# Layer 1 MLP of a diffusion backbone: the seven products of a pair in another order, and the low parts of the second weights made by an accumulating DMA

## The chip, the cores and the metric

The kernel runs on one core of one Trainium2 chip. The metric is the device time of one execution in microseconds (us), from the first to the last instruction of the core plus what the launch adds. The core has five engines that each run their own list of instructions strictly in order: PE (TensorE, matrix products), DVE (VectorE), ACT (ScalarE), POOL (GpSimd) and SP (SyncE, which here only issues DMAs). They wait for one another through semaphores. Sixteen DMA engines move data; SP and POOL issue into queues of their own.

## The reference, cut to what matters

Two groups of tokens (512 latent, 128 context, here joined to T = 640 columns) run through two layers. Each layer is a mixer and then an MLP; the change touches only the MLP of layer 1:

```python
def squared_relu_mlp(h, w1, w2):          # h (640, 1024), w1 (1024, 4096), w2 (4096, 1024)
    a = jax.nn.relu(h @ w1)
    return (a * a) @ w2
...
        x = x + g2 * squared_relu_mlp(h, w_ff1[l], w_ff2[l])
```

All data are float32. The kernel gets the precision by splitting each operand in two: a high part, which is the value rounded to the engine's float32r format, and a low part, which is the value less its high part.

## The kernel before

**Three matmuls for one.** `mm3` (lines 798 to 803) multiplies two split operands: high weights by high data (L801), high weights by low data (L802), low weights by high data (L803). So each weight tile is an SBUF tile `w` of 128 partitions by 2 by 1024: `w[:, 0]` high, `w[:, 1]` low. L803 is the only one of the three that reads the low part of the weights.

**Weights.** A `Weights` object `st` holds one list of weight tiles in the order of use. `loads` issues SP DMAs from DRAM into five buffers `raw` of 512 KB. `pump` takes the next item of the list: ACT rounds `raw` into the high part (L214) and DVE subtracts it from `raw` into the low part (L216). `need` returns a tile and pumps until it is there. `free` gives its place back. In this stage there are six places for converted tiles (eight, less two that hold sums of inputs): an item that finds no free place is not pumped, however often `pump` is called.

**The MLP of layer 1.** The 4096 hidden columns are worked in 8 blocks of 512 (`b` = 0 to 7). Blocks 0 and 1 make their hidden activations in the ordinary way before the stage that changes. For blocks 2 to 7, `up7` makes a pair of 128-column tiles, f and g, with two pairs to a block. It is a seven-product scheme in the manner of Strassen: the 2 by 2 products over the two halves of the 1024 inputs and the two halves of the tokens (`C1`, 320 columns each) are formed by 7 products in place of 8. Each product is 4 `mm3`, so 12 matmuls of 320 columns. Its weights ("w1s", items 0 to 6 of a pair) are f and g pieces or their sums, made by `w1s_use`: ACT rounds (L558), DVE makes the low part (L559), and for some items DVE then works the next combination into `raw` (L563). Two items share one place. `p1`, `u2`, `u3` are partial sums that ACT (L1598) and DVE (L1581) take out of the PSUM banks `pa`, `pb`, `pc`, `pd`; four of the products accumulate a second time into a bank that has been read. `finish` squares the rectified result into the split activations `aa`: ACT Relu (L1586), ACT Square (L1587), ACT Copy to the high part (L1588), DVE low part (L1589).

After its two pairs, a block's `down` multiplies its four activation tiles with the second weights and adds the result to `x` (L1407). Its 16 results (8 of rows `d`, 2 of columns) take 192 matmuls. The second weights of a block are four "w2" items, (k, h) with k = 0 or 2 and h the half of the output rows; all four places are taken while the block's `down` runs, and the two left are for w1s items. `blocks7` starts the block's `down` with "early" parts: the first two rows d for both column halves, on the first pair's activations alone (24 matmuls), then the second pair's part of them.

The order on each engine is the order in which this code issues instructions; `pump` calls, written by hand, place the conversions between the others.

Of the kernel before, what the change touches and what calls it, by code (L numbers as in the profile page):

```python
# [136 lines left out]
class Weights:  # L137
# [3 lines left out]
    def __init__(self, nc, raw):  # L141
        self.nc, self.raw = nc, raw
        self.items, self.loaded, self.done = [], 0, 0
        self.raw_live, self.raw_cap, self.tiles, self.of = 0, RAWB, {}, {}
        self.raws = {}
        self.slots = None
        self.caps = {}
        self.lo = nc.vector
        self.own = {}
        self.hold = None  # L150
        self.slow = ()
        self.later, self.skip = [], False
        self.keep, self.second = {}, None

# [39 lines left out]
    def pump(self, n=1):  # L194
# [4 lines left out]
        while n > 0 and self.done < len(self.items):  # L199
# [8 lines left out]
            if use is None:  # L208
                if own is None:
                    self.of[key], w = self.slots.take([128, 2, 1024], F32R)  # L210
                else:
                    w = own()
                r = ts[0][:, 0:size]
                self.nc.scalar.activation(out=w[:, 0, 0:size], in_=r, func=AF.Copy)  # L214
                lo = self.nc.gpsimd if key[0] in self.slow else self.lo
                lo.tensor_tensor(  # L216
                    out=w[:, 1, 0:size], in0=r, in1=w[:, 0, 0:size].bitcast(F32), op=ALU.subtract
                )
# [50 lines left out]
def body(ctx, tc, a):  # L269
# [278 lines left out]
    def w1s_use(l, b, p, i):  # L548


        def use(ts):
            if i == 0:
# [3 lines left out]
            src = (f0, g0, g0, f0, f1, g1, f1)[i]  # L556
# [4 lines left out]
                    4: (f1, f1, g0, ALU.subtract)}.get(i)  # L561
# [15 lines left out]
    def add_w2h(l, b):  # L577
        for h in range(2):
            for k in (0, 2):
                st.add(("w2", l, b, k, h), [(rows(a["w_ff2"][l], b * FB + k, 2, h * 512, 512), (2, 512))], 1024)  # L580
# [866 lines left out]
    def mlp(l, C, H, lead, CL, per_d, per_c, mid, tick=None, turn=None, seven=False):  # L1447
# [107 lines left out]
        def up7(b, p):  # L1555
            n = C[0][1]

            def product(i, op, ps, first):
# [9 lines left out]
                st.free(("w1s", l, b, p, i))  # L1568
# [14 lines left out]
            def finish(j, ci, src=None):  # L1583
                c = slice(*C[ci])
                r, aa = rs[j][:, c], A[b, j]
                act(out=r, in_=r if src is None else src, func=AF.Relu)  # L1586
                act(out=r, in_=r, func=AF.Square)  # L1587
# [11 lines left out]
            st.pump()  # L1599
            pd = product(1, 2, None, True)  # L1600
            st.pump()
# [9 lines left out]
            pa = product(4, (0, 1), pa, False)  # L1611
            lo()
            lo = finish(f, 0, pa)
            if not p:
                st.pump()
            pd = product(5, 3, pd, False)
# [3 lines left out]
            pc = product(6, (1, 1), pc, False)  # L1620
# [3 lines left out]
            lo()  # L1624
            if not p:
                st.pump()

        def blocks7(f0):

            for b in range(NFB):  # L1630
# [9 lines left out]
                if b < NFB - 1:  # L1640
                    early = cut(range(2), C) if b >= f0 else []
                    todo = [(d, c, None) for d in range(2 if early else 0, KD) for c in C]
                    for j, (d, c, ps) in enumerate(early + todo):
# [5 lines left out]
                        if j % 2 or j > 3:  # L1649
# [537 lines left out]
```

## Time and profile before

| | us |
|---|---|
| runs, median (lowest to highest of 3) | 1299.65 (1296.63 to 1301.23) |
| profiled execution, device time | 1302.88 |
| its span | 1301.1 |
| PE busy | 1261.8 (97%) |
| DVE busy | 826.6 (64%) |
| ACT busy | 549.3 (42%) |
| POOL busy | 216.5 (17%) |

The profiled execution is one run of its own, 3.2 us above the median of the others. PE is busy 97% of the span, with the caution that matmuls are pipelined and a record is longer than the distance to the next one. The stage that the change touches runs from about 960 us to the end.

### The profile page before, as it was taken

What the parts mean: (1) busy time and instruction counts of PE and PEld (TensorE: products, weight loads), DVE (VectorE), ACT (ScalarE), POOL (GpSimd) and SP (SyncE); (2) the same over time, 40 slices, a digit from 0 to 9 for tenths busy, and PEclk for the clock granted to TensorE, in tenths of its full rate; (3) what the DMA queues carried; (4) which work ended last, traced back from release to release, by engine and by line L of the source; (5) the groups of instructions that cost most, each with busy time, mean ns of one, the idle gap of its engine ahead of it and who ended that gap; (6) DMA issues with size and microseconds to landing.
All of it is one profiled execution on the core that took longest, in us unless ns stands there. A gap on an engine that the chain in (4) does not pass through costs nothing.

```text
span 1301.1 us, 20746 instructions
## 1 busy us (share of the span) xinstructions
PE 1261.8 (97%) x8308; PEld 1183.4 (91%) x8308; DVE 826.6 (64%) x1553; ACT 549.3 (42%) x993; POOL 216.5 (17%) x182
## 2 busy tenths in 40 slices
PE   7999999999999999999999999799999999999997
PEld 5899975689999999999999998789999999999997
DVE  5753864564766575666666638876887567675664
ACT  4445454453453434333343414534235435354353
POOL 0010312221113221313131315610000000000001
PEclk8999999999999999999999999899999999999999
DMA  7742286340335344444353431202113223132102
GB/s 291 261 164 72 81 227 234 131 170 25 116 117 160 113 145 131 150 126 157 119 161 114 147 130 33 97 1 79 52 35 112 80 67 98 38 111 84 61 33 82
DMA packets 63200, 149.89 MB, mean 115 GB/s; under 512 B 5072, under 2 KB 21968, under 8 KB 62592
## 3 DMA queue, kind: packets, MB, share of 16 engines
q1 hardware_dynamic: 61360, 142.53, 33.3%
q0 software_dynamic: 1456, 5.96, 1.9%
q8 instruction: 65, 1.06, 0.3%
q14 instruction: 31, 0.25, 0.1%
q10 hardware_dynamic: 288, 0.08, 0.0%
HBM read 140.02 MB, written 5.39 MB: 112 GB/s over the span
## 4 chain that ended last, share of the span: by engine, by line
PE 79%; DVE 10%; ACT 7%; issue 2%; DMA 1%; POOL 0%; DVEq 0%; ACTq 0%; POOLq 0%
PE dn_ps L802 11%; PE dn_ps L801 11%; PE dn_ps L803 11%; PE up_ps L801 7%; PE up_ps L803 7%; PE up_ps L802 7%; PE wo_ps L801 1%; PE o_ps L1302 1%; PE wo_ps L803 1%; PE wo_ps L802 1%; ACT r L1587 1%; DVE w L216 1%; ACT w L558 1%; ACT r L1586 1%; PE t_ps L1269 1%
## 5 line engine op out<-in xcount | busy, mean ns | idle before, releaser
L801 PE MATMUL dn_ps<-aa,w 128*128 128x320 f32 (+4 forms) x1024 | 319.1, 312 | 2.1 <-ACT aa L1588 2.1
L802 PE MATMUL dn_ps<-aa,w 128*128 128x320 f32 (+4 forms) x1024 | 318.4, 311 | 0.7
L803 PE MATMUL dn_ps<-aa,w 128*128 128x320 f32 (+4 forms) x1024 | 316.8, 309 | 0.0
L802 PE MATMUL up_ps<-h,w 128*128 128x320 f32 (+2 forms) x800 | 248.6, 311 | 6.0 <-DVE h L752 5.9
L801 PE MATMUL up_ps<-h,w 128*128 128x320 f32 (+2 forms) x800 | 249.6, 312 | 1.3 <-ACT h L748 1.3
L803 PE MATMUL up_ps<-h,w 128*128 128x320 f32 (+2 forms) x800 | 248.6, 311 | 0.0
L1407 DVE SCALAR_TENSOR_TENSOR x<-dn_ps,mod,x 128x320 f32<-128x320 f32 (+4 forms) x360 | 144.7, 434 | 115.0 <-PE dn_ps L803 113.2
L801 PEld LDWEIGHTS dn_ps<-aa,w 128*128 128x128 f32 x1024 | 193.1, 189 | 5.8 <-ACT aa L1588 4.1
L216 DVE TENSOR_TENSOR w<-raw,w 128x1024 fp32r<-128x1024 f32 (+4 forms) x122 | 151.3, 1250 | 70.9 <-ACT w L214 69.8
L802 PEld LDWEIGHTS dn_ps<-aa,w 128*128 128x128 f32 x1024 | 193.0, 188 | 2.5 <-DVE aa L1589 2.4
L803 PEld LDWEIGHTS dn_ps<-aa,w 128*128 128x128 f32 x1024 | 193.0, 189 | 0.0
L214 ACT ACTIVATE w<-raw 128x1024 fp32r<-128x1024 f32 (+4 forms) x131 | 132.0, 1026 | 112.0 <-DMA raw<-w_ff 85.0
L802 PEld LDWEIGHTS up_ps<-h,w 128*128 128x128 f32 x800 | 151.2, 189 | 8.1 <-DVE h L752 8.1
L801 PEld LDWEIGHTS up_ps<-h,w 128*128 128x128 f32 x800 | 151.0, 189 | 4.9 <-issue 3.4
L466 POOL TENSOR_TENSOR acc<-acc,raw 128x1024 f32<-128x1024 f32 x42 | 100.7, 2399 | 303.7 <-ACT raw L464 297.6
L803 PEld LDWEIGHTS up_ps<-h,w 128*128 128x128 f32 x800 | 151.0, 189 | 0.0
L559 DVE TENSOR_TENSOR w<-raw,w 128x512 fp32r<-128x512 f32 x84 | 57.7, 687 | 34.6 <-ACT w L558 33.7
L558 ACT ACTIVATE w<-raw 128x512 fp32r<-128x512 f32 x84 | 51.4, 624 | 61.9 <-DVE raw L563 57.1
L464 ACT ACTIVATE raw<-raw,cs 128x1024 f32<-128x1024 f32 x42 | 48.3, 1149 | 62.6 <-DVE acc L459 54.2
L1925 POOL TENSOR_TENSOR y<-y,fg 128x1024 f32<-128x1024 f32 x1 | 2.4, 2392 | 416.5 <-ACT y L1921 416.5
L1481 DVE TENSOR_TENSOR r<-r,up_ps 128x328 f32<-128x328 f32 (+2 forms) x80 | 37.6, 484 | 42.6 <-ACT r L1480 41.0
L1484 DVE TENSOR_TENSOR aa<-r,aa 128x640 fp32r<-128x640 f32 (+3 forms) x52 | 39.6, 762 | 35.6 <-ACT aa L1483 35.6
(404 smaller groups left out, 2122.1 us busy)
## 6 DMA issues: line engine op xcount, KB each, us to landing
raw<-w_ff SPq DMA_DIRECT2D x126, 512.0 KB, 3.6
raw<-w_mod SPq DMA_DIRECT2D x80, 512.0 KB, 3.9
raw<-w_m SPq DMA_DIRECT2D x16, 512.0 KB, 6.0
raw<-w_out SPq DMA_DIRECT2D x8, 512.0 KB, 4.4
kT<-ckvT POOLq DMA_DIRECT2D x4, 768.0 KB, 10.8
xr<-x SPq DMA_DIRECT2D x5, 512.0 KB, 5.5
xs<-x SPq DMA_DIRECT2D x2, 1280.0 KB, 9.3
x<-xs POOLq DMA_DIRECT2D x2, 1280.0 KB, 9.6
```

The source lines that it names most:

```text
L214: self.nc.scalar.activation(out=w[:, 0, 0:size], in_=r, func=AF.Copy)
L216: lo.tensor_tensor(out=w[:, 1, 0:size], in0=r, in1=w[:, 0, 0:size].bitcast(F32), op=ALU.subtract)
L464: act(out=raw if k else acc[1], in_=raw, func=AF.Copy, scale=w[1])
L466: nc.gpsimd.tensor_tensor(out=acc[1], in0=acc[1], in1=raw, op=ALU.add)
L558: act(out=w[:, 0], in_=src, func=AF.Copy)
L559: vec.tensor_tensor(out=w[:, 1], in0=src, in1=w[:, 0].bitcast(F32), op=ALU.subtract)
L801: mm(ps, lhsT=st_[0], rhs=mv[0], start=first, stop=False, skip_group_check=on)
L802: mm(ps, lhsT=st_[0], rhs=mv[1], start=False, stop=False, skip_group_check=on)
L803: mm(ps, lhsT=st_[1], rhs=mv[0], start=False, stop=last, skip_group_check=on)
L1407: vec.scalar_tensor_tensor(out=xv, in0=ps[:, p0:p0 + c1 - c0], scalar=gate[:, d, m:m + 1], in1=xv, op0=ALU.mult, op1=ALU.add)
L1481: vec.tensor_tensor(out=rv, in0=rv, in1=ps, op=ALU.mult)
L1484: vec.tensor_tensor(out=aa[:, 1, lo:hi], in0=r[:, lo:hi], in1=aa[:, 0, lo:hi].bitcast(F32), op=ALU.subtract)
```

## The change

It does five things, all in layer 1's MLP.

1. **Low parts of w2.** For the 32 w2 items (4 in each of 8 blocks), DVE's subtraction is gone. ACT writes the negated high part into the low part's place, and POOL then issues a DMA that adds the weights from DRAM onto it. The `raw` buffer is still loaded, for the high part.
2. **Order of the products.** The accumulating products come as pd, pc, pa in place of pa, pd, pc; so the items 4, 5 and 6 of a pair have other sources, and the last `finish` of a pair is that of (f, first columns).
3. **Pumps.** Two `pump` calls at a pair's start go, others move. In `down`, the 14 calls of a block are those with j > 1. A w1s item is freed one product later than before.
4. **`finish` from PSUM.** The product that is finished straight from PSUM is squared by DVE (Relu times PSUM) in place of ACT.
5. **Early parts** take the second half of the columns first.

```diff
@@ class Weights, pump
                 self.nc.scalar.activation(out=w[:, 0, 0:size], in_=r, func=AF.Copy)
+                if key in self.add_lo:
+                    self.nc.scalar.activation(
+                        out=w[:, 1, 0:size], in_=w[:, 0, 0:size].bitcast(F32), func=AF.Copy, scale=-1.0
+                    )
+                    src, shape = loads[0]
+                    v = w[:, 1, 0:size].rearrange("p (k n) -> p k n", k=shape[0])
+                    self.nc.gpsimd.dma_start(out=v, in_=src, accum_op=ALU.add)
                 lo = self.nc.gpsimd if key[0] in self.slow else self.lo
-                lo.tensor_tensor(
-                    out=w[:, 1, 0:size], in0=r, in1=w[:, 0, 0:size].bitcast(F32), op=ALU.subtract
-                )
+                if key not in self.add_lo:
+                    lo.tensor_tensor(
+                        out=w[:, 1, 0:size], in0=r, in1=w[:, 0, 0:size].bitcast(F32), op=ALU.subtract
+                    )
@@ w1s_use
-            src = (f0, g0, g0, f0, f1, g1, f1)[i]
+            src = (f0, g0, g0, f0, g1, g0, f1)[i]
...
-                    4: (f1, f1, g0, ALU.subtract)}.get(i)
+                    4: (g0, f1, g0, ALU.subtract)}.get(i)
@@ up7, product
-                st.free(("w1s", l, b, p, i))
+                gone.append(("w1s", l, b, p, i))
+                if i:
+                    st.free(gone.pop(0))
@@ up7, finish
-                act(out=r, in_=r if src is None else src, func=AF.Relu)
-                act(out=r, in_=r, func=AF.Square)
+                if src is not None:
+                    act(out=r, in_=src, func=AF.Relu)
+                    vec.tensor_tensor(out=r, in0=r, in1=src, op=ALU.mult)
+                else:
+                    act(out=r, in_=r, func=AF.Relu)
+                    act(out=r, in_=r, func=AF.Square)
@@ up7
             pa = product(0, (0, 0), None, True)
             p1 = new("p1")
             act(out=p1, in_=pa, func=AF.Copy)
-            st.pump()
             pd = product(1, 2, None, True)
-            st.pump()
             pb = product(2, 1, None, True)
...
-            pa = product(4, (0, 1), pa, False)
-            lo()
-            lo = finish(f, 0, pa)
-            if not p:
-                st.pump()
-            pd = product(5, 3, pd, False)
+            pd = product(4, 3, pd, False)
             add(out(g, 0), u2, pd)
             lo()
             lo = finish(g, 0)
-            pc = product(6, (1, 1), pc, False)
+            if not p:
+                st.pump()
+            pc = product(5, (1, 1), pc, False)
             add(out(f, 1), u2, pc)
             lo()
             lo = finish(f, 1)
-            lo()
             if not p:
                 st.pump()
+            pa = product(6, (0, 1), pa, False)
+            lo()
+            finish(f, 0, pa)()
+            st.free(gone.pop(0))
@@ blocks7
-                    early = cut(range(2), C) if b >= f0 else []
+                    early = cut(range(2), C[::-1]) if b >= f0 else []
...
-                        if j % 2 or j > 3:
+                        if j > 1:
                             st.pump()
```

In the built program the instructions come in another order on ACT and DVE. The rows below are of one block (b = 5) and its second pair; the other blocks from 2 to 7 read alike. Line numbers of the changed program are 10 to 20 higher than before: L215 is the old L214, L567 the old L558, L568 and L572 the old L559 and L563, L1596 the old L1581, L1606 to L1609 the old L1586 to L1589, L1618 the old L1598; L217 is the negated copy, L1603 and L1604 the Relu and the product of the new `finish`.

ACT before, from the second pair's `p1`: `w_11157`, `w_11177`, `w_11197` and `w_11221` are the four w2 tiles of the block, `up_ps` are PSUM banks, `r` and `aa` a tile before and after the split.

```order
L1598 ACTIVATE p1_11155<-up_ps_11142 128x320
L214 ACTIVATE w_11157<-raw_10687 128x1024
L214 ACTIVATE w_11177<-raw_10907 128x1024
L214 ACTIVATE w_11197<-raw_10909 128x1024
L1586 ACTIVATE r_11141<-r_11141 128x320
L1587 ACTIVATE r_11141<-r_11141 128x320
L1588 ACTIVATE aa_11140<-r_11141 128x320
L214 ACTIVATE w_11221<-raw_11136 128x1024
L1586 ACTIVATE r_11139<-up_ps_11142 128x320
```

ACT in the change, at the end of the same pair: `w_11200` holds the last two w1s items, `w_11276` and `w_11311` are the first two w2 tiles, and L1603 is the Relu of the pair's last product.

```order
L567 ACTIVATE w_11200<-raw_10803 128x512
L1606 ACTIVATE r_11154<-r_11154 128x320
L1607 ACTIVATE r_11154<-r_11154 128x320
L1608 ACTIVATE aa_11153<-r_11154 128x320
L1606 ACTIVATE r_11152<-r_11152 128x320
L1607 ACTIVATE r_11152<-r_11152 128x320
L1608 ACTIVATE aa_11151<-r_11152 128x320
L1603 ACTIVATE r_11152<-up_ps_11155 128x320
L1608 ACTIVATE aa_11151<-r_11152 128x320
L215 ACTIVATE w_11276<-raw_10816 128x1024
L217 ACTIVATE w_11276<-w_11276 128x1024
L215 ACTIVATE w_11311<-raw_10941 128x1024
```

Before, three of the four w2 tiles are converted near the start of the pair and the fourth before the last products; in the change the first stands behind the finish of the pair's last product.

DVE before, in the same pair: the low parts of the w2 tiles (L216) stand among the sums of products (L1581).

```order
L216 TENSOR_TENSOR w_11157<-raw_10687,w_11157 128x1024
L216 TENSOR_TENSOR w_11177<-raw_10907,w_11177 128x1024
L1581 TENSOR_TENSOR u2_11193<-p1_11155,up_ps_11180 128x320
L1581 TENSOR_TENSOR u3_11194<-u2_11193,up_ps_11164 128x320
L216 TENSOR_TENSOR w_11197<-raw_10909,w_11197 128x1024
L1581 TENSOR_TENSOR r_11141<-u3_11194,up_ps_11204 128x320
L216 TENSOR_TENSOR w_11221<-raw_11136,w_11221 128x1024
L1589 TENSOR_TENSOR aa_11140<-r_11141,aa_11140 128x320
```

DVE in the change, from the end of the first pair (`w_11111` holds items 3 and 4 of the second pair, `raw_10801` is the buffer in which combinations are made) to the second pair's `u3`:

```order
L568 TENSOR_TENSOR w_11111<-raw_10801,w_11111 128x512
L1596 TENSOR_TENSOR r_11022<-u2_11066,up_ps_11074 128x320
L1609 TENSOR_TENSOR aa_11023<-r_11024,aa_11023 128x320
L568 TENSOR_TENSOR w_11111<-raw_10803,w_11111 128x512
L572 TENSOR_TENSOR raw_10801<-raw_10803,raw_10801 128x4x128
L1609 TENSOR_TENSOR aa_11021<-r_11022,aa_11021 128x320
L1604 TENSOR_TENSOR r_11022<-r_11022,up_ps_11025 128x320
L1609 TENSOR_TENSOR aa_11021<-r_11022,aa_11021 128x320
L1596 TENSOR_TENSOR u2_11196<-p1_11168,up_ps_11183 128x320
L1596 TENSOR_TENSOR u3_11197<-u2_11196,up_ps_11170 128x320
```

The w2 subtractions are gone from DVE, and the first pair's conversions and low parts now stand ahead of the second pair's `u2` and `u3`; `u3` reads the bank `up_ps_11170`, into which the product right behind it accumulates again.

POOL had nothing to do in this stage before. In the change it has 32 rows such as these four of the block:

```order
L222 DMA w_11276<-w_ff2 128x2x512
L222 DMA w_11311<-w_ff2 128x2x512
L222 DMA w_11338<-w_ff2 128x2x512
L222 DMA w_11353<-w_ff2 128x2x512
```

Each waits for ACT's negated copy of its tile.

## Rows read from the trace of the kernel before

**Rows 1.** Head of the page: busy time of each engine (share, instructions).

```profile
PE 1261.8 (97%) x8308; PEld 1183.4 (91%) x8308; DVE 826.6 (64%) x1553; ACT 549.3 (42%) x993; POOL 216.5 (17%) x182
```

**Rows 2.** Timeline of PE in block 4's `down`: start, length, line, tiles.

```profile
1100.31 0.31 PE L803 MATMUL dn_ps<-aa,w 128*128 128x320 f32 x1
...
1121.86 0.31 PE L803 MATMUL dn_ps<-aa,w 128*128 128x320 f32 x1
```

**Rows 3.** Timeline of PE: the same place in blocks 5 and 6 (wait in brackets).

```profile
1153.54 0.41 PE L801 MATMUL dn_ps<-aa,w 128*128 128x320 f32 x1 [0.26 <-ACT aa L1588]
...
1207.58 0.42 PE L801 MATMUL dn_ps<-aa,w 128*128 128x320 f32 x1 [0.27 <-ACT aa L1588]
```

**Rows 4.** Waits of PE from 960 to 1280 us: total, times, longest.

```profile
PE up_ps L801 <- DVE u L1581: 2.4, 2, 1.5
PE dn_ps L801 <- ACT aa L1588: 2.1, 7, 0.6
PE up_ps L801 <- DVE x L1407: 0.5, 1, 0.5
```

**Rows 5.** Timeline of DVE at the end of block 4's second pair.

```profile
1092.97 0.48 DVE L1581 TENSOR_TENSOR r<-u,up_ps 128x320 f32<-128x320 f32 x1
1095.94 1.23 DVE L216 TENSOR_TENSOR w<-raw,w 128x1024 fp32r<-128x1024 f32 x1 [2.49 <-ACT w L214]
```

**Rows 6.** ACT's groups, 1019 to 1235 us: count, busy, mean ns, idle before.

```profile
L558 ACT ACTIVATE w<-raw 128x512 fp32r<-128x512 f32 x57 | 34.9, 625 | 45.2 <-DVE raw L563 41.4 <-PE dn_ps L803 3.8
L214 ACT ACTIVATE w<-raw 128x1024 fp32r<-128x1024 f32 x16 | 16.0, 1048 | 0.0
L1588 ACT ACTIVATE aa<-r 128x320 fp32r<-128x320 f32 x32 | 15.1, 472 | 1.0
...
L1598 ACT ACTIVATE p<-up_ps 128x320 f32<-128x320 f32 x9 | 3.9, 429 | 63.0 <-PE up_ps L803 63.0
L1586 ACT ACTIVATE r<-up_ps 128x320 f32<-128x320 f32 x8 | 3.4, 419 | 0.0
```

**Rows 7.** DVE's groups in the same window.

```profile
L559 DVE TENSOR_TENSOR w<-raw,w 128x512 fp32r<-128x512 f32 x56 | 38.5, 687 | 21.3 <-ACT w L558 20.6
L563 DVE TENSOR_TENSOR raw<-raw 128x512 f32<-128x512 f32 x32 | 22.0, 689 | 0.5
L216 DVE TENSOR_TENSOR w<-raw,w 128x1024 fp32r<-128x1024 f32 x16 | 19.2, 1222 | 12.3 <-ACT w L214 12.3
L1589 DVE TENSOR_TENSOR aa<-r,aa 128x320 fp32r<-128x320 f32 x32 | 15.6, 488 | 12.9 <-ACT aa L1588 12.9
L1581 DVE TENSOR_TENSOR r<-u,up_ps 128x320 f32<-128x320 f32 x24 | 11.5, 480 | 0.0
```

**Rows 8.** DMA issues, whole span: engine, count, KB each, median us to landing.

```profile
raw<-w_ff SPq DMA_DIRECT2D x126, 512.0 KB, 3.6
...
cnt<-cnt POOLq DMA_DIRECT2D x1, 64.0 KB, 4.7
```

**Rows 9.** Line 1401's two POOL loads (`x<-xs`, 1280 KB each): landing.

```profile
DMA to landing us min/median/max: 8.5/9.6/10.8
```

**Rows 10.** Line 1108's two POOL copies (`kT<-ckvT`, 768 KB each): landing.

```profile
DMA to landing us min/median/max: 6.3/9.3/12.3
```

**Rows 11.** Stretches: us, PE busy, PEld, DVE, ACT, POOL, granted clock (share of full), DMA share, GB/s.

```profile
842.00:844.00 2.00, 0.00 (x0) 0.00 (x0) 2.00 (x2) 0.70 (x2) 1.08 (x1) 1.00 0.00 0
844.00:852.00 8.00, 7.70 (x42) 7.70 (x43) 6.32 (x14) 2.94 (x7) 0.00 (x0) 0.79 0.01 2
153.60:155.60 2.00, 0.11 (x2) 0.06 (x1) 2.00 (x3) 0.07 (x1) 1.12 (x1) 1.00 0.00 0
156.00:164.00 8.00, 7.61 (x28) 6.96 (x27) 5.94 (x13) 1.94 (x6) 2.52 (x4) 0.57 0.49 114
```

**Rows 12.** Timeline of PE inside the second of these stretches.

```profile
846.20 0.47 PE L801 MATMUL up_ps<-h,w 128*128 128x320 f32 x1
846.46 0.47 PE L802 MATMUL up_ps<-h,w 128*128 128x320 f32 x1
```

More of the change, by code (lines that the diff above doesn't have):

```diff
@@ L153, in __init__ @@
         self.keep, self.second = {}, None
+        self.add_lo = set()
     def add(self, key, loads, size, use=None):
@@ L579, in add_w2h @@
             for k in (0, 2):
+                st.add_lo.add(("w2", l, b, k, h))
                 st.add(("w2", l, b, k, h), [(rows(a["w_ff2"][l], b * FB + k, 2, h * 512, 512), (2, 512))], 1024)
@@ L1556, in up7 @@
             n = C[0][1]
+            gone = []
             def product(i, op, ps, first):
```

## The prediction

> **What bounds the kernel now.** The page's busy line comes first: PE works in 97% of the span [rows 1], so an edit gains only where PE waits, and loses wherever it makes PE wait. The timeline of PE gives its pace: from 1100.31 to 1121.86 us stand 148 matmuls with no wait, 147 steps of 0.1466 us [rows 2]. A block from 2 to 7 has 2 pairs of 7 products of 12 matmuls, and 192 in `down`: 360, or 52.8 us. From one block to the next the same matmul starts 54.0 us later (1153.54 to 1207.58) [rows 3]. So a middle block loses 1.2 us and no more. The waits of PE say at what [rows 4]: at the start of the second pair's part of `down`, seven waits of 2.1 us in all for ACT's `aa`; in the first block 2.4 us for DVE's `u` and 0.5 for DVE's `x`. Behind them is DVE's queue: at 1095.94 it has stood idle for 2.49 us with a w2 subtraction at its head that waits for ACT's rounding, and the sums of finished products are queued behind it [rows 5]. All that the change can gain in this stage is 6 x 1.2 + 2.9, with 0.4 more for the last block, whose wait of 0.6 is longer than the others: 10.5 us.
>
> **Part 1, the low parts of w2.** DVE loses 32 subtractions of 1.22 us [rows 7]; that is its 39 us, but only the 10.5 us above are PE's. ACT gains 32 copies of 128 x 1024. The nearest row is the rounding of the same size, 1.05 us [rows 6]. What decides is where these stand, and the order of the built program tells it. Before, the w2 tiles of a block are rounded along the second pair. In the change, the places are filled by w1s items earlier, two pumps are gone, and the first w2 tile is pumped only when `down` asks for it. ACT's row for it (L215) then stands behind the finish of the pair's very last product. ACT works in order, so nothing of `down` can start before. Three waits of PE follow in each block.
>
> First, the pair boundary. The fifth product of the second pair accumulates in the bank pd, which `u3` must have read. From the end of the first pair's fourth product, ACT and DVE hand over to each other down to that `u3`: add 0.48, Relu, Square and Copy 1.41, rounding of item 2 0.62, its low part 0.69, combination 0.69, add 0.48, three ACT steps 1.41, rounding 0.62, low part 0.69, add 0.48, three ACT steps 1.41, rounding 0.62, low part 0.69, combination 0.69, low part of `aa` 0.49, product 0.48, copy 0.47, `p1` 0.43, `u2` 0.48, `u3` 0.49 [rows 6, 7]: 13.8 us, some 14.1 with handovers. PE has seven products between, 7 x 1.76 = 12.3. It waits about 1.8 us; bounds 0 (if enough of the chain overlaps) and 2.3.
>
> Second, the start of `down`. From that `u3`: low part 0.69, add 0.48, three ACT steps 1.41, rounding of item 6 0.62, low part 0.69, add 0.48, three ACT steps for g and three for f 2.82, Relu 0.42, product 0.48, copy 0.47, rounding of the first w2 tile 1.05: 9.6, and 9.9 with handovers. PE has three products in it, 5.3 us, and stands until the high part is there: 4.3 us too long (4.0 to 4.6). What was late before, `aa`, now hides inside this wait.
>
> Third, the low part. PE does two matmuls (0.29 us) and comes to the first that reads it. ACT's negated copy ends 1.05 us after the high part, then POOL issues the DMA. PE waits 0.8 us plus the DMA's time L. Queued behind this matmul is the whole of `down`, so DVE's `x` and the next conversions wait too; nothing covers it.
>
> No row shows an accumulating DMA. From below, L is that of SP's plain load of the same 512 KB, 3.6 us [rows 8]. From POOL's queue there are 64 KB in 4.7 [rows 8] and 1280 KB in 8.5 at the least [rows 9], which on a line give 6.1 us for 512 KB; if the bytes count twice, since the destination is read as well, 7.7. The last of POOL's copies of 768 KB, with the others ahead of it, took 12.3 [rows 10], the upper end. I take 7.0, between 6.1 and 7.7.
>
> The Trainium skill's page "DMA: Bandwidth & Descriptors" (section "Anatomy of one DMA — SWDGE (gpsimd) path") fits a DMA issued by GpSimd with 2.0 us plus bytes over 436 GB/s, so 3.2 us for 512 KB as an estimate. It gives 5.0 us for the 1280 KB that took 8.5 to 10.8 here [rows 9], so the trace does not agree. By the page's figure the sum below would end at 1363 us.
>
> The second w2 tile is rounded and negated 2.1 us later than the first and its DMA issued so much later; PE needs its low part 24 matmuls (3.5 us) after the first one's. The tiles of the other half are needed 72 matmuls later still. If the DMAs don't queue for each other, they cost nothing.
>
> **The clock.** After 2 us or more without matmuls the granted clock fell to half twice: no matmul ran from 842 to 844 us, and in the next 8 us the mean is 0.79; two ran from 153.6 to 155.6, and from 156 to 164 the mean is 0.57 [rows 11]. With 1.2 GHz at 0.50 that is 3.4 and 6.9 us at the lower level, in which a matmul comes every 0.26 to 0.27 us [rows 12] in place of 0.147. Each us at it loses 0.45: 1.5 and 3.1 us. The change leaves PE idle for 4.3 us and then nearly 8, so I count this once in each block, 2.3 us, the mean.
>
> **The other parts.** The new product order lets the fifth product start on pd in place of pa; its cost is the first wait above. Squaring by DVE in 12 pairs costs 0.48 for ACT's 0.47 and stands in the chains above. The early parts in the other column order ask for `aa` that is long finished when the low part arrives: nothing. In blocks 0 and 1 the w2 tiles are converted among ordinary work, 96 matmuls (14 us) or more before their use, so their DMAs lie beside PE's work; with L over 14 us that cover would be gone. SP issues the same loads; those of w1s items that wait for the later w2 rounding are for the next block, a whole `down` (28 us) away.
>
> **Sum.** A block from 2 to 7 loses 1.8 + 4.3 + 0.8 + 7.0 + 2.3 = 16.2 us, six of them 97.2; less the 10.5 us of waits that go, 86.7. The profiled execution of before took 1302.9, so 1389.6; the median of the runs lies 3.2 below that execution, so I predict **1386 us**.
>
> With all low bounds a block loses 0 + 4.0 + 0.8 + 3.6 + 1.5 = 9.9: 1348 us. With all high ones 2.3 + 4.6 + 0.8 + 12.3 + 3.1 = 23.1: 1428 us.
>
> **The rivals.**
>
> *Slow accumulation.* The four DMAs of a block share the engines with four loads of SP that come free at the same time, and read as well as write. If one takes 16 us rather than 7, a block loses 25.2, and the second tile, queued behind the first, some 3 more: 6 x 28 - 10.5 is 158, so 1457 us. It is this case where L passes 12.3, the longest POOL row. For it: each of POOL's copies behind one another took longer, 6.3 to 12.3 us [rows 10]. Against it: in this stage POOL's queue is empty before each block.
>
> *Faster.* If the first w2 tile were ready when `down` starts, PE would wait for neither ACT nor the DMA, and DVE's relief would count in full: 1302.9 - 10.5 - 3.2 = 1289 us. For it: DVE did hold up the sums [rows 5], and ACT is busy only 42% of the span [rows 1]. Against it: ACT's order. It decides only if the tile's rounding and negation came L + 1.1 us before the pair's last product ends, and in the program they stand behind it.
>
> *The accumulation is hidden.* If the DMA took hardly more than its issue, some 1 us, and the clock stayed up, a block would lose 1.8 + 4.3 + 0.8 + 1 = 7.9: 6 x 7.9 - 10.5 = 37, so 1337 us. Against it: the plain load of the same bytes takes 3.6 us [rows 8].
>
> **Chances.** The forecast 0.82 (with its own range 1348 to 1428), slow accumulation 0.11, hidden accumulation 0.03, faster 0.04. The range goes from 1350 to 1435 us, which takes in the nearer part of the slow case. Within 0.3% of 1299.65 (about what a measurement of this kernel can tell from no change) little can end: the faster case gives faster 0.03 and same 0.01, since its gain is only 0.8%, and the others slower 0.96.
>
> **What the changed kernel's profile would show.** In the waits of PE: six long ones of `mm3`'s third line (803 before) for a DMA `w<-w_ff`, 7 to 9 us each with the 0.8, and six of about 4 us of the first line for ACT's w2 rounding; some 2 us at the second pair's fifth product for DVE's `u`. The period of a block 68 to 71 us. Clock at 0.50 behind each long wait, for 3 to 7 us. DVE less busy by 39 - 6 = 33 us, ACT busier by about 28. The page's DMA issues with 32 more rows on POOL's queue and a median near 7 us.
>
> I am wrong in size if L is not near 7: each us of it is 6 us of the time. I am wrong in kind if PE's first wait in `down` is short, which would mean that ACT reached the w2 tile while products were still running.

## The result, and the profile after

The changed kernel takes 1397.49 us (median of 4 runs, 1395.16 to 1403.61) against 1300.44 us for the kernel before beside it (4 runs, 1296.63 to 1301.3): a ratio of 1.076, 95% interval 1.0719 to 1.08. It is slower by 97 us; the forecast was 1386 us. Its profiled execution has a span of 1396.1 us, 95.0 more than that of before.

The head of the page answers to [rows 1]:

```profile
PE 1282.9 (92%) x8308; PEld 1206.7 (86%) x8308; DVE 795.7 (57%) x1533; ACT 576.6 (41%) x1013; POOL 254.9 (18%) x214
```

DVE lost 31 us of work and ACT gained 27 (33 and 28 were forecast), and PE, with the same 8308 matmuls, fell from 97% to 92% of a longer span. Off-loading DVE worked, and it isn't what the time hangs on. Where PE stands now is in its waits from 940 to 1390 us (total, times, longest), which answer to [rows 4]:

```profile
PE dn_ps L813 <- DMA w<-w_ff: 51.4, 6, 9.2
PE dn_ps L811 <- ACT w L215: 17.2, 6, 3.8
PE up_ps L811 <- DVE u L1596: 11.5, 6, 2.0
PE up_ps L811 <- DVE x L1417: 1.2, 1, 1.2
```

The three waits of the forecast are there, once in each of the 6 blocks: 80.1 us against 6 x 13.9 = 83.4. One block as the timeline of PE shows it (block 3; the two rows at 1062 are the high weights, the next is the first that reads the low part):

```profile
1052.35 0.39 PE L811 MATMUL up_ps<-w 128*128 128x320 f32 x1 [1.90 <-DVE u L1596]
...
1062.10 0.41 PE L811 MATMUL dn_ps<-aa,w 128*128 128x320 f32 x1 [2.69 <-ACT w L215]
1062.36 0.30 PE L812 MATMUL dn_ps<-aa,w 128*128 128x320 f32 x1
1071.84 0.60 PE L813 MATMUL dn_ps<-aa,w 128*128 128x320 f32 x1 [9.18 <-DMA w<-w_ff]
...
1072.51 0.47 PE L812 MATMUL dn_ps<-aa,w 128*128 128x320 f32 x1
1072.77 0.47 PE L813 MATMUL dn_ps<-aa,w 128*128 128x320 f32 x1
```

The timeline of ACT ahead of it shows the order that the forecast read from the built program: the last `aa` of the pair (L1608), and only then the w2 tile's rounding and its negated copy.

```profile
1060.63 0.47 ACT L1608 ACTIVATE aa<-r 128x320 fp32r<-128x320 f32 x1 [0.63 <-DVE r L1604]
1061.01 1.04 ACT L215 ACTIVATE w<-raw 128x1024 fp32r<-128x1024 f32 x1
1062.08 1.06 ACT L217 ACTIVATE w<-w 128x1024 fp32r<-128x1024 f32 x1
```

POOL issues the tile's DMA at 1063.44, which takes it 1.20 us, and the data lands at 1071.8. The clock, in stretches with the columns of [rows 11], falls twice in the block:

```profile
1050.00:1052.00 2.00, 0.45 (x4) 0.19 (x2) 1.43 (x4) 1.31 (x3) 0.00 (x0) 1.00 0.00 0
...
1054.00:1056.00 2.00, 2.00 (x9) 2.00 (x8) 0.73 (x2) 1.21 (x3) 0.00 (x0) 0.50 0.71 249
...
1070.00:1072.00 2.00, 0.16 (x1) 0.19 (x2) 0.00 (x0) 0.00 (x0) 0.74 (x1) 0.50 1.11 244
1072.00:1074.00 2.00, 2.00 (x8) 2.00 (x9) 0.00 (x0) 0.00 (x0) 0.00 (x0) 0.50 1.11 230
1074.00:1076.00 2.00, 2.00 (x10) 2.00 (x9) 0.00 (x0) 0.00 (x0) 0.00 (x0) 0.50 1.09 230
...
1078.00:1080.00 2.00, 2.00 (x15) 2.00 (x15) 0.90 (x3) 0.00 (x0) 0.00 (x0) 1.00 1.11 267
```

PE is as busy at 0.50 as at 1.00, but the rows count 8 to 10 matmuls in 2 us, against 15 in the last one. Last, what moved the bytes (DMA issues of the whole span, as in [rows 8]; the first row is that of SP's plain loads):

```profile
raw<-w_ff SPq DMA_DIRECT2D x126, 512.0 KB, 3.7
...
w<-w_ff POOLq DMA_DIRECT2D x32, 512.0 KB, 8.3
```

### The profile page after: what moved, and what is told of

Same layout as the page of the kernel before. It is cut to its first block, busy times and chain, and to the rows that moved or that the text cites. A ratio compares the mean times of both kernels' runs of the same rounds, so it can differ in the third digit from the quotient of the medians.

```text
span 1396.1 us, 20889 instructions
## 1 busy us (share of the span) xinstructions
PE 1282.9 (92%) x8308; PEld 1206.7 (86%) x8308; DVE 795.7 (57%) x1533; ACT 576.6 (41%) x1013; POOL 254.9 (18%) x214
## 3 DMA queue, kind: packets, MB, share of 16 engines
q8 instruction: 66, 1.08, 0.3%
## 5 line engine op out<-in xcount | busy, mean ns | idle before, releaser
L813 PE MATMUL dn_ps<-aa,w 128*128 128x320 f32 (+4 forms) x1024 | 323.4, 316 | 51.4 <-DMA w<-w_ff 51.4
L811 PE MATMUL dn_ps<-aa,w 128*128 128x320 f32 (+4 forms) x1024 | 324.9, 317 | 17.2 <-ACT w L215 17.2
L812 PE MATMUL dn_ps<-aa,w 128*128 128x320 f32 (+4 forms) x1024 | 323.2, 316 | 0.0
L1417 DVE SCALAR_TENSOR_TENSOR x<-dn_ps,mod,x 128x328 f32<-128x328 f32 (+5 forms) x360 | 145.5, 435 | 219.7 <-PE dn_ps L813 218.6
L812 PE MATMUL up_ps<-h,w 128*128 128x320 f32 (+2 forms) x800 | 251.3, 314 | 5.2 <-DVE h L762 5.2
L811 PE MATMUL up_ps<-h,w 128*128 128x320 f32 (+2 forms) x800 | 252.9, 316 | 1.3 <-ACT h L758 1.3
L813 PE MATMUL up_ps<-h,w 128*128 128x320 f32 (+2 forms) x800 | 251.4, 314 | 0.0
L813 PEld LDWEIGHTS dn_ps<-aa,w 128*128 128x128 f32 x1024 | 198.4, 194 | 53.0 <-issue 46.0
L811 PEld LDWEIGHTS dn_ps<-aa,w 128*128 128x128 f32 x1024 | 198.5, 194 | 20.6 <-ACT w L215 18.8
L812 PEld LDWEIGHTS dn_ps<-aa,w 128*128 128x128 f32 x1024 | 198.2, 194 | 0.1
L215 ACT ACTIVATE w<-raw 128x1024 fp32r<-128x1024 f32 (+4 forms) x131 | 133.0, 1025 | 108.6 <-DMA raw<-w_ff 83.1
L812 PEld LDWEIGHTS up_ps<-h,w 128*128 128x128 f32 x800 | 154.2, 193 | 6.6 <-DVE h L762 6.4
L811 PEld LDWEIGHTS up_ps<-h,w 128*128 128x128 f32 x800 | 154.2, 193 | 4.9 <-issue 3.4
L813 PEld LDWEIGHTS up_ps<-h,w 128*128 128x128 f32 x800 | 153.6, 192 | 0.0
L225 DVE TENSOR_TENSOR w<-raw,w 128x1024 fp32r<-128x1024 f32 (+4 forms) x90 | 112.7, 1259 | 44.3 <-ACT w L215 43.1
L222 POOL DMA_DIRECT2D w<-w_ff x32 | 38.6, 1205 | 451.9 <-ACT w L217 450.6
L567 ACT ACTIVATE w<-raw 128x512 fp32r<-128x512 f32 x84 | 50.6, 620 | 99.0 <-DVE raw L572 97.4
L568 DVE TENSOR_TENSOR w<-raw,w 128x512 fp32r<-128x512 f32 x84 | 57.8, 688 | 52.4 <-ACT w L567 51.2
```

Of the source, the lines that this page charges most:

```text
L222: self.nc.gpsimd.dma_start(out=v, in_=src, accum_op=ALU.add)
L225: lo.tensor_tensor(out=w[:, 1, 0:size], in0=r, in1=w[:, 0, 0:size].bitcast(F32), op=ALU.subtract)
L567: act(out=w[:, 0], in_=src, func=AF.Copy)
L568: vec.tensor_tensor(out=w[:, 1], in0=src, in1=w[:, 0].bitcast(F32), op=ALU.subtract)
L811: mm(ps, lhsT=st_[0], rhs=mv[0], start=first, stop=False, skip_group_check=on)
L812: mm(ps, lhsT=st_[0], rhs=mv[1], start=False, stop=False, skip_group_check=on)
```

## The experiments

**Theory**: placement. A w2 tile that ACT reaches only behind the pair's last finish puts rounding, negation and DMA one behind the other, bare on PE's path; where products cover them they cost little. **R1**: an accumulating DMA costs its time wherever it stands. **R2**: the product order alone costs. **R3**, on the DMA's length: the accumulation itself makes it long. Ratios are to the kernel before on the same chip; its median read 1300.17 to 1303.38 us beside the different kernels, so a difference between two times below is good to some 3 us. Lines of `mm3` and of the other functions shift by a line or two from kernel to kernel; the third matmul is the one for which a DMA or a low part is waited for.

**Without the DMAs.** DVE subtracts again; the rest as changed.

```diff
-                st.add_lo.add(("w2", l, b, k, h))
```

> The changed kernel with DVE's subtraction back in place of ACT's negated copy and the accumulating DMA; product order, pumps, finish and early parts as changed. My theory (the places and the pumps of the new order make the waits, and the DMA is one of three that then lie bare on PE's path): the waits of about 2 us at the pair boundary (for DVE's u) and of 2.7 to 4.3 us at the start of down (for ACT's w2 rounding) stay, 6 times each, and the third shrinks from about 8.7 us to about 1 us (one DVE subtraction of 1.22 us less two matmuls); the half-clock stretch behind it goes. That is 2 + 4 + 1 + 1.4 = 8 to 9 us in each of 6 blocks less some of the waits of before: 1337 to 1350 us. Rival R1 (the accumulating DMA alone costs, wherever it stands): about the time of before, 1295 to 1305 us, with no wait of 2 us left. Rival R2 (the product order alone costs): no lower than 1385 us.

Measured: 1348.19 us, ratio 1.0348 (1.0329 to 1.0368). The waits of PE in the same stretch:

```profile
PE dn_ps L810 <- ACT w L215: 17.3, 6, 3.8
PE up_ps L810 <- DVE u L1595: 11.5, 6, 2.0
PE dn_ps L812 <- DVE w L225: 5.3, 7, 1.5
```

The first two waits are those of the changed kernel to 0.1 us; only the third fell, 51.4 to 5.3. So the DMA is worth 49 of the 97 us, and the other 48 have nothing to do with it: R1 can't be the whole story, and neither can R2, which asked for 1385 us or more here. One thing I expected didn't come: the half-clock stretch in `down` didn't go with the long wait (in block 3, 21 steps in 5.60 us from 1052.30), so the time lies at the top of my range.

**Half the DMAs.** From block 2 on only the tiles of the second half of the output rows keep theirs.

```diff
-                st.add_lo.add(("w2", l, b, k, h))
+                if h or b < 2:
+                    st.add_lo.add(("w2", l, b, k, h))
```

> The changed kernel in which, for blocks 2 to 7, only the two w2 tiles of the second half of the output rows (the third and fourth of a block) keep the accumulating DMA; the first and second are subtracted by DVE. The DMAs left are needed 72 matmuls (10.6 us) or more after the first ones, at the same rate of POOL and of the DMA engines per tile. My theory (a DMA costs only where nothing covers it): they cost nothing, so the time is that of the changed kernel without any of them, 1348 us measured, within 4 us: 1344 to 1352 us, and no wait of PE for a w2 DMA over 1 us. Rival R1 (an accumulating DMA costs wherever it stands): 12 of the 24 remain, so half of the 49 us between the two: about 1372 us.

Measured: 1347.23 us, ratio 1.0347 (1.033 to 1.0364), the same as with no DMA at all (1348.19), and PE waits for none, though their median landing, 9.4 us, is longer than the changed kernel's 8.3. R1 asked for 1372 us. What a DMA costs here is its place.

**The DMAs alone, in the old kernel.** Items, `pump`, products and finish as before, plus part 1 of the change.

```diff
+                if key in self.add_lo:
+                    self.nc.scalar.activation(
+                        out=w[:, 1, 0:size], in_=w[:, 0, 0:size].bitcast(F32), func=AF.Copy, scale=-1.0
+                    )
...
+                    self.nc.gpsimd.dma_start(out=v, in_=src, accum_op=ALU.add)
...
+                st.add_lo.add(("w2", l, b, k, h))
```

> The kernel before with only the low parts of w2 changed: ACT's negated copy and the accumulating DMA on all 32 tiles; products, pumps, finish and early parts as before. My theory: three of a block's four w2 tiles are converted in the middle of the second pair, so their DMAs lie beside products, and only the last-converted tile's DMA can be bare at the third matmul of down: a wait of 2 to 4 us in each of 6 blocks, and less of DVE's 1.2 us: 1309 to 1322 us. Rival R1 (an accumulating DMA costs its 8 us wherever it stands, or ACT and the DMA engines pay for it): a bare wait of 8 to 9 us in each block, 1350 to 1360 us. If all of it were hidden: 1289 to 1297 us.

Measured: 1312.43 us, ratio 1.0076 (1.0054 to 1.0098), inside my range. The waits of PE at the third matmul:

```profile
PE dn_ps L813 <- ACT r L1597: 8.4, 3, 3.8
PE dn_ps L813 <- DMA w<-w_ff: 5.2, 3, 2.6
```

Both rows are the same matmul, three blocks each. It doesn't read `r`; where several semaphores are waited for, the profile names the one that moved last, so I count both for the DMA: 13.6 us, 2.3 to 3.8 in five blocks and 0.2 in the last, against 8.6 a block in the changed kernel. In block 3 the DMA was issued at 1036.07, 5.2 us ahead of `down`'s first matmul, and the matmul started at 1044.39: the same 8.3 us, mostly under products. In block 4, where the row names `r`, the two are 1093.22 and 1101.29, 8.1 us apart. The range held, but not for my reason: the tile that PE waits for is the first one converted, not the last, since even the first is issued only some 5 us ahead.

**The pumps put back**, with the DMAs and without.

```diff
             act(out=p1, in_=pa, func=AF.Copy)
+            st.pump()
             pd = product(1, 2, None, True)
+            st.pump()
             pb = product(2, 1, None, True)
```

> The changed kernel with the two pump calls at a pair's start put back, the accumulating DMAs kept. My theory: ACT reaches the w2 tiles in the middle of the second pair again, so that wait and DMA at the start of down shrink from 2.7 + 8.7 us to 1 to 3 us together, the pair-boundary wait stays or grows to 2 to 4 us (ACT's two more 1.05 us steps a tile stand in its chain): 1325 to 1335 us. Rival R1 (the DMA costs wherever it stands): no change, 1390 to 1400 us. Rival R2 (the product order costs): 1380 to 1400 us, with the wait at the pair boundary the largest.

Measured: 1339.35 us, ratio 1.028 (1.0261 to 1.03), 4 us above my range. Two calls are worth 58 us of the 97. Waits of PE:

```profile
PE dn_ps L813 <- DMA w<-w_ff: 12.5, 4, 4.1
PE up_ps L811 <- DVE u L1596: 9.1, 12, 2.7
PE dn_ps L813 <- ACT r L1606: 8.4, 2, 4.3
```

The wait for ACT's rounding at the start of `down` is gone (in the last block 1.6 us for `aa` are left) and that at the third matmul is 20.9 us in place of 51.4; it was up to 4.3 us a block, more than the 3 I allowed. The wait at the pair boundary, which I expected to stay or grow, fell from 1.9 us to 1.0 or less.

> The changed kernel with the two pump calls at a pair's start put back and with DVE's subtraction in place of the accumulating DMA: what is left of the change is the product order, the later freeing, the finish from PSUM by DVE and the early parts. My theory: the wait at the start of down is gone, that at the pair boundary for DVE's u is the one left and grows, since w2 roundings and subtractions stand in its chain again: 3 to 4.5 us in each of 6 blocks with a half-clock stretch of 1 to 1.5 us behind some: 1320 to 1335 us; so with the pumps back the DMAs cost 5 to 15 us (1339 us with them), without them 49. Rival R2' (the product order costs nothing by itself, only the missing pumps do): 1300 to 1306 us. Rival R1: 1290 to 1300 us, as much below 1339 us as the changed kernel without DMAs was below 1397 us.

Measured: 1334.39 us, ratio 1.0248 (1.0228 to 1.0268). One kind of wait is left in these blocks, at the fifth product: 4.0 us in each second pair, 2.7 in the first pair of block 2 and some 0.2 in the other first pairs.

```profile
PE up_ps L810 <- DVE u L1595: 28.0, 12, 4.1
```

Together the four kernels make a table (us): without the two pumps 1397 with the DMAs and 1348 without; with them 1339 and 1334. The DMAs cost 49 us in the one place and 5 in the other. The 5 are a balance: with the pumps back, the DMAs take the waits for `u` from 28.0 to 9.1 us, which is the relief of DVE, and add 20.9 at the third matmul. Taken one after the other, the 97 us are 31 for the product order with the small parts, 14 for the missing pumps and 49 for the DMAs; the 3 that are missing lie within the spread of the kernel before.

**What makes a DMA long.** The DMA copies and doesn't add.

```diff
-                    self.nc.gpsimd.dma_start(out=v, in_=src, accum_op=ALU.add)
+                    self.nc.gpsimd.dma_start(out=v, in_=src.bitcast(F32R))
```

> The changed kernel whose 32 POOL DMAs copy the weights into the low part's place and don't accumulate (so the low part is the whole weight): same queue, bytes, issue and place. It tells what the accumulation itself adds to a DMA of 512 KB from POOL. If the destination's read counts (R3): the landing falls from a median of 8.3 us to about 6 us, the third wait from 8.7 us to about 6.5 us, and the time by 6 x 2.3 = 14 us to about 1383 us. If the time is that of a POOL DMA of 512 KB beside SP's loads whatever it does: within 3 us of the changed kernel, 1394 to 1400 us, and a landing of 8 us or more. If it falls to the 3.6 us of SP's plain loads: 6 x 4.7 = 28 us, 1369 us.

Measured: 1385.6 us, ratio 1.0641 (1.0611 to 1.0671), 12 us below the changed kernel. Over all 32 DMAs the median landing is 6.9 us, and the third wait 42.3 us, 7.1 a block: near the 6 and 6.5 of the case that the destination's read counts. POOL's issue takes 0.71 us, not 1.20. Landing of the four DMAs of one block (min, median, max), in block 3 and in block 7, for which no next weights are loaded; first the copying kernel, then the changed one:

```profile
DMA to landing us min/median/max: 6.9/7.8/8.3
...
DMA to landing us min/median/max: 3.9/4.5/4.8
```

```profile
DMA to landing us min/median/max: 8.3/10.6/13.9
...
DMA to landing us min/median/max: 5.9/6.7/8.3
```

Both causes are there, and neither alone: accumulating adds 2.2 to 2.8 us to the median, and blocks with SP's loads beside the four have 3.3 to 3.9 more than the one without. The first is shown by the edit, the second by comparing blocks; no run took SP's loads away. The loads pay too; in the changed kernel from 1060 to 1090 us:

```profile
raw<-w_ff SPq DMA_DIRECT2D x4, 512.0 KB, 12.6
w<-w_ff POOLq DMA_DIRECT2D x4, 512.0 KB, 10.6
```

Landing of SP's loads (min, median, max) around the start of block 3's `down`, first in the kernel without the DMAs (1030 to 1080 us), then in the copying kernel (1053 to 1064 us), then in the changed kernel (1060 to 1072 us):

```profile
DMA to landing us min/median/max: 3.5/3.7/5.4
...
DMA to landing us min/median/max: 3.7/8.3/9.9
...
DMA to landing us min/median/max: 3.7/12.6/14.9
```

The copying and the changed kernel issue the four loads in the same rhythm, one in 2.03 us, so the 4.3 us between their medians come from the accumulation. Without the DMAs the loads are less crowded, and how much of the first step is their own crowding no run separates. Loads and DMAs start together for a reason: each rounding of a w2 tile frees its `raw` buffer, so in the changed kernel SP's loads are issued at 1062.07, 1064.11, 1066.14 and 1068.17 us, each 1.4 us ahead of one of POOL's DMAs (1063.44 and so on).

The Trainium skill's page "DMA: Bandwidth & Descriptors" (section "Issuing engines are not separate DMA queues") says that DMAs of all issuing engines run on the same 16 DMA engines and interleave there. The trace agrees: beside each other both kinds land later, the loads in 12.6 us for 3.7 and POOL's in 10.6 for 6.7. The DMA share doesn't tell the two cases apart: it is 1.09 to 1.12 from 1070 to 1080 us, and 0.97 to 1.13 from 1349 to 1357 us, where POOL's four are the only ones.

**The product order alone, and the small parts alone**, each put on the kernel before.

```diff
-            pa = product(4, (0, 1), pa, False)
-            lo()
-            lo = finish(f, 0, pa)
-            if not p:
-                st.pump()
-            pd = product(5, 3, pd, False)
+            pd = product(4, 3, pd, False)
...
+            pa = product(6, (0, 1), pa, False)
+            lo()
+            finish(f, 0, pa)()
```

> The kernel before with only the product order changed (accumulating products pd, pc, pa with the sources of items 4 to 6, the finish of f's first columns last): DVE subtracts w2, ACT squares, places are freed at once, pumps and early parts are as before. My theory: the fifth product accumulates in pd, which u3 must have read, and the w2 roundings and subtractions stand ahead of u2 and u3, so PE waits 3.5 to 4.5 us at each second pair's fifth product and there is a half-clock stretch behind some: the 1320 to 1336 us of the kernel with all but DMAs and missing pumps (1334 us measured). Rival (the order itself is free, and the finish by DVE, the late freeing or the early parts cost the 31 us): 1300 to 1306 us.

Measured: 1328.19 us, ratio 1.0212 (1.0182 to 1.0241). Waits of PE:

```profile
PE up_ps L801 <- DVE u L1581: 22.3, 12, 3.3
```

The place is the expected one: the second pair's fifth product waits for `u3`, 3.29 us in block 3, a little under the 3.5 to 4.5 I expected (1.9 in block 2, whose first pair waits 2.7; the other first pairs wait 0.2 to 0.3). So R2 holds for less than a third of the loss.

```diff
+                    act(out=r, in_=src, func=AF.Relu)
+                    vec.tensor_tensor(out=r, in0=r, in1=src, op=ALU.mult)
...
+                gone.append(("w1s", l, b, p, i))
+                if i:
+                    st.free(gone.pop(0))
...
+                    early = cut(range(2), C[::-1]) if b >= f0 else []
...
+                        if j > 1:
```

> The kernel before with only the small parts of the change: DVE squares what is finished from PSUM, a w1s place is freed one product later, the early parts take the second half of the columns first, and 14 pumps of down stand at j over 1; products, pumps at a pair's start and DVE's w2 subtractions as before. As I priced them in the prediction (at nothing): 1300 to 1306 us. Rival: in the product order of before, the last product's results are f's second columns, so early parts that take these first wait for their low part, and DVE's product stands behind a w2 subtraction: 2 to 3 us in each of 6 blocks, 1312 to 1322 us; then these parts are free only together with the new product order.

Measured: 1320.65 us, ratio 1.0161 (1.013 to 1.0191): the rival, not my price of nothing. Waits of PE:

```profile
PE up_ps L801 <- DVE u L1584: 10.5, 7, 2.2
PE dn_ps L801 <- ACT aa L1595: 7.6, 6, 1.6
```

The second row is the early parts that ask for the columns finished last. In the new order those are finished before the other half, and the changed kernel has no such wait. The first row is the sixth product (of each second pair, and once of a first pair), which accumulates in pd and needs `u3`; which of the small parts delays it wasn't separated. The 28 and 20 us of the two don't add: both together, with subtraction and pumps as before, are the 31 us of the kernel above (1334.39).

**A version that beats both?** In the old kernel only the first tile's DMA was waited for, so I left it to DVE (`if h or k:` ahead of `add_lo.add`), and in a second kernel the first two (`if h:`).

> The kernel before in which the second, third and fourth w2 tile of each block get their low parts by accumulating DMA, and only the first is subtracted by DVE. With all four, PE stood for the first tile's DMA alone, 2 to 3 us in each of 6 blocks. The second tile's DMA is issued 2 us behind the first and its low part is needed 24 matmuls (3.5 us) behind the first one's, so with the first wait gone it can be late by about 0.5 to 1.2 us. My theory: 0 to 6 us below the kernel before of the same chip, with waits of PE for the DMA of 1.2 us at most. Rival R1: three quarters of the 9.4 us, about 7 us above it.

Measured: 1311.85 us, ratio 1.0069 (1.0052 to 1.0087): a miss, and R1's number. But the waits are of one kind and place, PE for the second tile's DMA:

```profile
PE dn_ps L814 <- DMA w<-w_ff: 7.7, 5, 1.9
```

Its DMA in block 4 was issued at 1094.90 and PE went on at 1105.53, 10.6 us later. I had reckoned with 8 to 9 us; the median of all 24 is 10.5. PE reads the second low part 3.5 us after the first, and these 2 us are bare. Behind two of the five waits there is a half-clock stretch as well, for some 4 us in all.

> The kernel before in which only the third and fourth w2 tile of each block (the second half of the output rows) get their low parts by negation and accumulating DMA. My theory: these are needed 72 matmuls (10.6 us) or more after the first tile, their DMAs of 8 to 9 us are issued before down begins, so no wait of PE is added; DVE loses 2 subtractions of 1.22 us in each block, ACT gains two copies of 1.06 us, and of the 1.2 us that a block lost before, a half or more goes: 3 to 7 us below the kernel before of the same chip, 1296 to 1300 us where that is 1303. Rival R1 (the DMA costs wherever it stands): half of the 9.4 us that all 32 of them cost in the kernel before, so 4 to 5 us above it.

Measured: 1297.27 us (6 runs, 1292.33 to 1298.06), ratio 0.9953 (0.9937 to 0.997): faster than the kernel before by 0.5%. Waits of PE from 960 to 1280 us:

```profile
PE up_ps L812 <- DVE u L1592: 2.8, 3, 1.5
PE dn_ps L812 <- ACT aa L1599: 0.2, 1, 0.2
```

The 2.1 us for `aa` of [rows 4] are 0.2, no wait for a DMA is there, and DVE's busy time is 810.0 us. From one block's `down` to the next (blocks 4 and 5) are now 53.3 us, against the 54.0 of [rows 3]:

```profile
1091.68 0.31 PE L812 MATMUL dn_ps<-aa,w 128*128 128x320 f32 x1
...
1144.98 0.31 PE L812 MATMUL dn_ps<-aa,w 128*128 128x320 f32 x1
```

Here the off-loading that the changed kernel spent in the wrong place gives 0.7 of the 1.2 us of a block. R1 predicted a loss.

## Why the prediction was right, by its steps

**What bounds the kernel, and the 10.5 us to be gained.** Right: an unloaded DVE is worth only what PE waits for it. The version above, with DVE relieved of half of the w2 subtractions, took 6.1 us off the median. In its profiled execution this stage is 4.0 us shorter (335.5 us for 339.5); the stage also starts 2.8 us earlier there, and no row ties that to the edit.

**The start of `down` stands behind ACT.** Right in place and kind; shown by the pumps, which remove that wait and most of the DMA's behind it and bring 58 us. The size was 2.9 us a block, not 4.3. The chain of ACT and DVE was priced well: from the fifth product's first matmul to `down`'s are 9.75 us in block 3, for 9.6 to 9.9. (The 4.3 left out the 0.3 us of handovers that the pair boundary's sum has.) The step that failed there is the one that let PE's three products take 5.3 us: after the wait at the pair boundary PE runs at half clock for some 3 us (1053.90 to 1057.10 in block 3, 12 matmuls in 3.20 us), so they take 1.4 us longer, while ACT's and DVE's steps keep their length (0.47 us for L1608 at 1054.25). In block 4 PE keeps its pace there, and its wait is longer, with 9.3 us from one to the other:

```profile
1123.89 0.39 PE L811 MATMUL up_ps<-w 128*128 128x320 f32 x1 [1.93 <-DVE u L1596]
...
1133.19 0.63 PE L811 MATMUL dn_ps<-aa,w 128*128 128x320 f32 x1 [3.77 <-ACT w L215]
```

**The pair boundary.** 1.8 us forecast, 1.9 measured.

**The third matmul.** 0.8 + 7.0 us forecast, 8.6 measured (51.4 over 6), so L was 7.8 on average. I had put the plain DMA at 6.1 us by a line through other POOL rows [rows 8, 9] and 7.7 if the bytes count twice. That line was wrong in its reason, and that 7.0 came near is in part luck: with no load of SP beside it, the accumulating DMA is quicker (5.9 us for the first tile of block 7) than 7.7, and in blocks 2 to 6, beside SP's loads, slower (7.9 to 8.3 for the first of the four). The sharing, which I had kept for the rival of 16 us, acts in every block but the last, in which PE waited 6.72 us. The second tile's DMA, priced at nothing, isn't waited for; but in block 3 PE came to its low part 6.3 us after the first one's and not 3.5, since it ran at half clock between. At full pace the 9.9 us since the issue would hardly have been enough, as an estimate by the 10.6 us that such a DMA took in the median there.

The Trainium skill's page "DMA: Bandwidth & Descriptors" (section "Anatomy of one DMA — SWDGE (gpsimd) path"), which the prediction set against the trace, is nearer than I held: with no load of SP beside it a plain copy landed in 3.9 us at the least, of which 0.71 is POOL's issue, against the page's 3.2 us. The fit that I took from it has no term for the accumulation or the sharing, and with its 3.2 us the sum would have been 34 us too low.

**The clock.** 2.3 us a block for one stretch; there are two. From 1072.24 to 1077.57 us 20 matmuls take 5.33 us in place of 2.93, a loss of 2.4, as priced (1.3 to 2.4 in the six blocks); the stretch behind the pair boundary costs 1.4 more in block 3 (and about as much in four other blocks; not in block 4). I had counted only gaps of 2 us or more, but one of my own two rows was shorter: in the stretch from 153.6 us of [rows 11] the kernel before shows this wait, with the half clock behind it:

```profile
155.55 0.41 PE L801 MATMUL gm_ps<-vn,w 128*128 128x320 f32 x1 [1.89 <-DVE qt L1068]
```

So the 1.8 us that I forecast for the pair boundary should have carried a stretch of their own. From 1062.10 to 1345.41 us (four blocks) the mean period is 70.8 us. Less 52.8 of matmuls that is 18.0, of which the view of waits has 13.9; some 3.2 are steps at half clock and 0.9 stand at the edges of waits, where a row's start lies further from the next than its wait says. I counted 2.3 for all that the waits don't show; it was 4.1.

**The sum.** Between the two profiled executions the time grew by 95.0 us, against 86.7 forecast. The waits came out at 80.1 us for 83.4, and that they are so near is luck in part: L was 0.8 us a block too short and the start of `down` 1.4 too long. What the waits don't show was 1.8 us a block too little, 6 x 1.8 = 10.8. The two make 7.5 of the 8.3 us. The other 3 of the 11.5 us between 1386 and 1397.5 come from the step to the median: I took off the 3.2 us by which the profiled execution of before lies above its median, but the changed kernel's (1397.83) lies only 0.3 above its own. The terms that were mis-sized are the clock, of which the stretch behind the pair boundary was left out, and the edges of the waits, which had no term.

**The other parts.** Nothing, I said; in the changed order no wait of their own is seen, but alone they cost 20 us. The price held for the combination, not for the parts: with the new order they add 3 us (31 for 28).

**The rivals.** Slow accumulation had a mechanism that acts, the sharing with SP's loads, but 16 us for L where 7.8 was measured. The faster case failed at its stated point: the tile is rounded behind the last product. Hidden accumulation fell with the median landing of 8.3 us.

## What to carry to other kernels

Before moving work off an engine that isn't the bound, ask where its replacement stands and how long its latency is: an operation of 1.2 us that is replaced by copy, issue and an 8 us DMA has to begin that much earlier, and the place is decided by what frees buffers and who pumps. Give the long-latency form to the tiles that are needed last, the short one to those needed first: in the old order of products this kernel gained 0.5% with half of the tiles in each form, and lost 0.7% with three of four and 0.8% with all of them in the long-latency one; in the changed order, which has other costs too, it lost 7.6% with all. Price a transfer with those that start beside it: here the same roundings that let POOL issue its DMAs freed the buffers for SP's loads. And price a gap in PE with the half-clock stretch that can follow it.

## What the runs showed of the hardware

- Behind a wait of PE of 1.9 to 2.0 us at the pair boundary the granted clock went to 0.50 for some 3 us in five of the six blocks, in block 3 when PE was busy again (1052.35 to 1053.9 us at full pace, then half); in block 4, behind 1.93 us, it stayed at 1.00.
- An accumulating DMA of 512 KB takes POOL 1.20 us to issue, a plain one 0.71. Issued four in a row, 2.0 us apart, they land in 6.7 and 4.5 us (medians of the four in block 7), beside four loads of SP in 10.6 and 7.8 (block 3), and those loads in 12.6 beside the accumulating DMAs, 8.3 beside the plain ones.
